# Four edits between the sub-layers of a two-layer trunk: tiles of their own for some weights, remainders on another engine, and the order of the norm's rows and squares

## The chip, the cores and the metric

The program runs on one core of a Trainium2 chip. The core has a matmul engine (PE, with weight loads shown apart as PEld), three engines for elementwise work (DVE or VectorE, ACT or ScalarE, POOL or GpSimd) and a queue that issues all transfers (SP). The metric is device time in microseconds (us) of one execution. The profile's times are counted from the first instruction of one profiled execution.

## The reference, cut to what matters

The trunk has two layers. Each has two sub-layers, a token mixer and an FFN, and around each stands a norm before and a norm behind:

```python
for l in range(DEPTH):
    h = _rmsnorm(x, pre_mix_norm[l])
    h = _hybrid_mixer(h, ...)
    x = x + _rmsnorm(h, post_mix_norm[l])
    h = _rmsnorm(x, pre_ffn_norm[l])
    h = _conv_glu_ffn(h, ffn_up[l], ffn_conv[l], ffn_conv_bias[l], ffn_down[l])
    x = x + _rmsnorm(h, post_ffn_norm[l])
```

`x` is 512 tokens by 1024 features in float32. The mixer's last step is a matmul with `w_out` (1024x1024), the FFN's first one is `ffn_up` (1024x5632) and its last one `ffn_down` (2816x1024). `_rmsnorm` divides each token's row by the root of its mean square, so nothing can be normed before the last feature of the matmul ahead of it is summed. That is the place the change is about: three transitions (mixer to FFN, FFN to the next layer's mixer, mixer to FFN) and the end of the program.

## The kernel before, in words

Features lie on the 128 partitions, tokens on the free axis. A weight unit is a tile of 128x1024 float32 numbers. It is loaded into one of two buffers `raw` (line 242), split by ACT into a rounded high half `whi` (line 146, 1 us) and by DVE or POOL into a remainder `wlo = raw - whi` (line 150). The pairs `whi`, `wlo` rotate through HL = 4 slots; a slot is free again once the matmuls have read the unit. An activation `hx` is split in the same way, and each product takes three matmuls (line 137): high by high, high by low, low by high.

**The transition.** A sub-layer's output has eight feature tiles `m` (`out_rows`). The last three of the mixer, and the last one of the FFN, are the *tail*: they are computed in two halves of 256 tokens, so that the norm of the first half can start while PE does the second. The steps of one half are: ACT squares the tail's sum into `vh` and DVE adds it to `acc`; PE sums `acc` over partitions (`pso<-cc,acc`); DVE and POOL make the inverse root (`rtp`); PE spreads it over the partitions (`pso<-cc,rtp`), and ACT copies it to the row `rs`. Then come eight rows `m` (function `row`): multiply by `rs` (tiles `A`, `B`, `C`, `psg`; DVE), add to `x` (tile `xt`; POOL for m = 1, 3, 5, else DVE), the high half of the next operand `hx` (ACT) and its low half (DVE, line 164). ACT also squares the new `x` for the norm that comes next (`sq`), and POOL adds the squares up (`acc<-acc,sq`).

The next sub-layer opens with its *lead*: three weight units into three PSUM tiles `pss`, half by half, while the operand tiles `hx` appear one by one. In the FFN of the profile these are 3 units x 8 tiles x 3 matmuls of 256 columns per half; in the mixer 16 small matmuls with `was` come to each half. The next norm's row (`rt`) is applied only when `pss` is read out. Behind the lead, PE goes on with units of 512 columns into four buffers `psg`.

**What sets the order.** The program is written out by a planner, `_Sched`: generators yield times, each operation has a cost, and the order in which they come out is the order on each engine. On the chip each engine works its list off in that order and waits for semaphores. So a change of costs or times in the planner moves instructions, and the chip's durations decide what these lists then wait for. In the planner a load lands 3.2 us after its issue. Around the transition the splitter sends a remainder to DVE or POOL, whichever is free sooner by the planner's count.

## Time and profile before

| | us |
|---|---|
| median of 3 runs | 1456.89 |
| the 3 runs | 1458.82, 1444.82, 1456.89 |
| the profiled execution | 1446.95 |
| its span, first to last instruction | 1445.2 |
| PE busy in it | 1388.6 |
| DVE busy | 949.3 |
| ACT busy | 610.1 |
| POOL busy | 593.2 |

The profiled execution is its span and 1.75 us around it. It is 9.94 us shorter than the median of the three runs, which lie 14 us apart. Busy times are sums over the whole span; the three transitions are about 30 us each, so a share of the span says little about them, and they are read from the timelines of the single engines.

### The profile page before, as it was taken

The numbers are of one execution on the slowest core, as the hardware profiler recorded it, in microseconds if no ns is written. First come the engines' busy times: TensorE is split into PE (matmuls) and PEld (weight loads), VectorE is DVE, ScalarE is ACT, GpSimd is POOL, SyncE is SP. The second block draws the span as 40 slices with busy tenths as digits, with TensorE's granted clock in tenths as the row PEclk, the third lists the DMA queues.
The fourth block names the chain that finished last, engine by engine and source line by source line (L and its number), as shares of the span: only waits on it lengthen the run. The fifth ranks groups of instructions, "written<-read, shape, count | busy, mean of one in ns | idle before, by whom it ended". The sixth has DMA issues, their size and how long they took to land.

```text
span 1445.2 us, 18826 instructions
## 1 busy us (share of the span) xinstructions
PE 1388.6 (96%) x7174; PEld 1147.8 (79%) x7174; DVE 949.3 (66%) x1503; ACT 610.1 (42%) x992; POOL 593.2 (41%) x359
## 2 busy tenths in 40 slices
PE   8999999998999999999999999999989999999996
PEld 5778766877888888888887877668878888888886
DVE  4785477667788788831379745668487888777213
ACT  4453356444544443332245434565355434443220
POOL 3344255314554444423343542543164544443332
PEclk9999999999999999999999999999999999999998
DMA  5233111032233223343332330110413333223331
GB/s 196 73 91 86 60 30 48 12 130 75 88 92 99 88 88 94 93 122 97 92 109 93 106 90 27 50 38 16 146 45 102 96 97 100 88 88 106 110 91 59
DMA packets 48698, 123.15 MB, mean 85 GB/s; under 512 B 15584, under 2 KB 18400, under 8 KB 48608
## 3 DMA queue, kind: packets, MB, share of 16 engines
q1 hardware_dynamic: 48608, 121.95, 27.7%
q8 instruction: 57, 0.93, 0.3%
q14 instruction: 33, 0.27, 0.1%
HBM read 115.11 MB, written 6.82 MB: 84 GB/s over the span
## 4 chain that ended last, share of the span: by engine, by line
PE 84%; DVE 12%; ACT 2%; issue 1%; DMA 0%; SPq 0%; POOL 0%; DVEq 0%; ACTq 0%
PE psg L137 70%; PE pss L137 9%; PE pso L137 2%; DVE kT L164 2%; DVE xt L150 1%; PE pss L142 1%; DVE A L150 1%; PE psg L142 1%; DVE hx L164 1%; DVE zt L150 1%; DVE qraw L164 1%; DVE C L150 1%; DVE rab L150 0%; DVE acc L150 0%; ACT whi L146 0%
## 5 line engine op out<-in xcount | busy, mean ns | idle before, releaser
L137 PE MATMUL psg<-hx,whi 128*128 128x512 f32 (+1 forms) x2080 | 629.0, 386 | 0.9 <-DVE C L157 0.8
L150 POOL TENSOR_TENSOR wlo<-raw,whi 128x1024 fp32r<-128x1024 f32 (+1 forms) x153 | 382.6, 2511 | 518.3 <-ACT whi L146 493.6
L137 PEld LDWEIGHTS psg<-hx,whi 128*128 128x128 f32 x2080 | 378.2, 189 | 78.2 <-issue 4.5
L137 PE MATMUL psg<-hx,wlo 128*128 128x512 f32 (+1 forms) x1040 | 396.2, 381 | 0.0
L146 ACT ACTIVATE whi<-raw 128x1024 fp32r<-128x1024 f32 (+1 forms) x208 | 215.5, 1036 | 262.9 <-PE psg L137 197.6
L164 DVE SCALAR_TENSOR_TENSOR B<-A,vv,B 128x510 f32<-128x510 f32 (+1 forms) x176 | 275.4, 1566 | 76.6 <-ACT B L146 73.5
L137 PEld LDWEIGHTS psg<-hx,wlo 128*128 128x128 f32 x1040 | 196.1, 189 | 38.0
L137 PE MATMUL psg<-hid,whi 128*128 128x512 f32 (+1 forms) x792 | 221.9, 366 | 0.0
L137 PEld LDWEIGHTS psg<-hid,whi 128*128 128x128 f32 x792 | 143.1, 189 | 24.3
L137 PE MATMUL psg<-hid,wlo 128*128 128x512 f32 (+1 forms) x396 | 144.8, 366 | 0.0
L150 DVE TENSOR_TENSOR wlo<-raw,whi 128x1024 fp32r<-128x1024 f32 (+1 forms) x55 | 70.6, 1286 | 109.0 <-ACT whi L146 108.9
L137 PE MATMUL psg<-whi,hx 128*128 128x512 f32 x384 | 123.7, 404 | 0.3 <-DVE A L150 0.3
L150 POOL TENSOR_TENSOR acc<-acc,sq 128x256 f32<-128x256 f32 (+1 forms) x65 | 68.1, 1048 | 103.8 <-ACT sq L146 100.7
L146 ACT ACTIVATE hid<-C 128x512 fp32r<-128x512 f32 x44 | 27.7, 630 | 179.5 <-DVE C L150 179.5
L137 PE MATMUL pss<-hx,whi 128*128 128x256 f32 (+1 forms) x336 | 82.3, 335 | 18.8 <-DVE hx L164 16.8
L137 PEld LDWEIGHTS psg<-hid,wlo 128*128 128x128 f32 x396 | 74.6, 189 | 12.2 <-POOL wlo L150 0.3
L137 PEld LDWEIGHTS pss<-hx,whi 128*128 128x128 f32 x336 | 61.9, 215 | 27.1 <-DVE hx L164 20.9
L146 ACT ACTIVATE B<-A,vv 128x512 f32<-128x512 f32 x88 | 71.0, 809 | 25.5 <-DVE A L150 24.5
L137 PEld LDWEIGHTS psg<-whi,hx 128*128 128x128 f32 x384 | 69.8, 190 | 13.6 <-DVE A L150 0.8
L137 PE MATMUL psg<-wlo,hx 128*128 128x512 f32 x192 | 75.7, 394 | 0.0
L150 DVE TENSOR_TENSOR A<-psg,rs 128x512 f32<-128x512 f32 x100 | 68.2, 683 | 2.0 <-POOL A L157 1.6
L137 PE MATMUL psg<-bT,bT 64*128 64x512 f32 (+3 forms) x128 | 48.2, 477 | 6.9 <-DVE nm L1170 4.2
(226 smaller groups left out, 1668.0 us busy)
## 6 DMA issues: line engine op xcount, KB each, us to landing
raw<-in_w_up_dram SPq DMA_DIRECT2D x88, 512.0 KB, 3.5
raw<-in_w_cm_dram SPq DMA_DIRECT2D x32, 512.0 KB, 3.6
raw<-in_w_dn_dram SPq DMA_DIRECT2D x32, 512.0 KB, 3.6
raw<-in_w_tm_dram SPq DMA_DIRECT2D x24, 512.0 KB, 3.5
raw<-in_w_o_dram SPq DMA_DIRECT2D x16, 512.0 KB, 3.5
raw<-in_w_dn_dram SPq DMA_DIRECT2D x16, 384.0 KB, 3.1
xt<-in_xT_dram SPq DMA_DIRECT2D x7, 512.0 KB, 6.7
scr_a<-am SPq DMA_DIRECT2D x8, 256.0 KB, 2.7
```

Source lines behind the costliest of these rows:

```text
L137: pe.matmul(ps, lhsT, rhs, start=start, stop=stop)
L142: pe.transpose(dst[:, i * P:(i + 1) * P], s, ident)
L146: nc.scalar.activation(out_, in_, func, **kw)
L150: (nc.vector if eng == "dve" else nc.gpsimd).tensor_tensor(out_, a, b, op=op)
L164: nc.vector.scalar_tensor_tensor(out_, a, s, b, op0=op0, op1=op1)
```

## The change

It has five parts. (1) Three weight units per layer, the lead of the FFN, get tiles of their own (`home`: the places of three mixer tiles that are done with once the scan is over), and the last unit of the FFN's down matmul gets a new tile `xu` of 2 x 768 columns; these four don't take a slot of the four. (2) From the end of the tail until the lead is done (`sc.chain`) every weight remainder goes to DVE. (3) The rows of a half start 1.1 us apart in the planner, not 0.6. (4) The squares for the next norm wait in the planner until all eight rows of their half are out. (5) The scratch of 16 KB per partition for another kind of transfer, of which the trace has none, is cut to 4 KB, to make room for `xu`.

```diff
@@ wseq
+        for i, tag in enumerate(("s7", "s5", "s1")):
+            home[len(wseq) + i] = (tag, (l, "scan", NC - 1))
         wseq += [(w_up[l, m], 1024) for m in range(2 * KF)]
...
+        home[len(wseq) - 1] = ("xu", None)
@@ splitter
-            yield from sc.get("wu", HL)
+            if u in home:
+                tag, flag = home[u]
+                if flag is not None:
+                    yield from sc.wait(flag)
+                if tag == "xu":
+                    pair = xp.tile([P, 2, 768], F32R, tag="xu", name="wxu")
+                else:
+                    pair = sp.tile([P, 2, 1024], F32R, tag=tag, name="whome")
+                hi, lo = pair[:, 0], pair[:, 1]
+            else:
+                yield from sc.get("wu", HL)
...
-            if len(wunit) > 1:
+            if sc.chain:
+                eng = "dve"
+            elif len(wunit) > 1:
                 eng = yield from sc.idle(("dve", "pool"), 1.5)
@@ square_sum
+        if key != "in":
+            yield from sc.wait(("rows", key, t0))
@@ lead
+        if last:
+            sc.chain = False
@@ out_rows, row
             left["m"] -= 1
+            left[t0] = left.get(t0, 8) - 1
+            if not left[t0]:
+                sc.set(("rows", key, t0))
@@ out_rows, chain
-                sc.spawn(row(m, seg, tail, r), 0, at=r + 0.6 * m)
+                sc.spawn(row(m, seg, tail, r), 0, at=r + 1.1 * m)
...
             sc.spawn(chain(seg, tail), 0)
+            sc.chain = True
@@ kernel
-    nc = _bacc.Bacc("TRN2", target_bir_lowering=False, num_devices=1)
+    nc = _bacc.Bacc("TRN2", target_bir_lowering=False, num_devices=1, dynamic_dma_scratch_size=4096)
```

How this moves instructions is seen at two transitions. The first is mixer to FFN in layer 0; the one in layer 1 differs from it in a few places only. On DVE, from the row `rs` of the first half to the first low half `hx`, there stood before:

```order
L150 TENSOR_TENSOR acc<-acc,vh 128x256
L150 TENSOR_TENSOR A<-A,rs 128x256
L150 TENSOR_TENSOR B<-B,rs 128x256
L157 TENSOR_SCALAR C<-psg,vv 128x256
L150 TENSOR_TENSOR C<-C,rs 128x256
L150 TENSOR_TENSOR xt_2717<-xt_2717,A 128x256
L150 TENSOR_TENSOR A<-A,rs 128x256
L150 TENSOR_TENSOR B<-B,rs 128x256
L150 TENSOR_TENSOR xt_2719<-xt_2719,C 128x256
L150 TENSOR_TENSOR acc<-acc,vh 128x256
L150 TENSOR_TENSOR C<-C,rs 128x256
L164 SCALAR_TENSOR_TENSOR hx_2842<-xt_2717,vv,hx_2842 128x256
```

And now:

```order
L151 TENSOR_TENSOR wlo<-raw,whi 128x1024
L151 TENSOR_TENSOR A<-A,rs 128x256
L151 TENSOR_TENSOR acc<-acc,vh 128x256
L151 TENSOR_TENSOR B<-B,rs 128x256
L151 TENSOR_TENSOR xt_2717<-xt_2717,A 128x256
L151 TENSOR_TENSOR wlo<-raw,whi 128x1024
L151 TENSOR_TENSOR C<-C,rs 128x256
L151 TENSOR_TENSOR acc<-acc,vh 128x256
L165 SCALAR_TENSOR_TENSOR hx_2842<-xt_2717,vv,hx_2842 128x256
```

Two remainders stand among the first rows (a third follows six instructions after the first `hx`), fewer rows are begun before the first `hx`, and the last addition to `acc` of the second half stands ahead of it.

On PE, the lead of the first half at the same transition (`pss_3065`, `3066`, `3067` are the three units' sums before; the rows go from the third quarter of the half on):

```order
L137 MATMUL pss_3065<-hx1_2843,whi_2854 128x256 x2
L137 MATMUL pss_3065<-hx1_2843,wlo_2855 128x256
L137 MATMUL pss_3066<-hx1_2843,whi_2966 128x256 x2
L137 MATMUL pss_3066<-hx1_2843,wlo_2967 128x256
...
L137 MATMUL pso_3109<-cc_80,rtp_3108 128x128 x2
L137 MATMUL pss_3067<-hx0_2842,whi_3006 128x256 x2
L137 MATMUL pss_3067<-hx0_2842,wlo_3007 128x256
```

The change's rows from the end of the tail on (`pss_3054`, `3055`, `3056` are the three units):

```order
L138 MATMUL pso_3074<-cc_80,acc_2622 128x1 x2
L138 MATMUL pss_3054<-hx0_2842,whome_2854 128x256 x3
L138 MATMUL pss_3055<-hx0_2842,whome_2880 128x256 x3
...
L138 MATMUL pss_3056<-hx0_2842,whome_2930 128x256 x6
L138 MATMUL pso_3074<-cc_80,rtp_3073 128x128 x2
L138 MATMUL pss_3054<-hx0_2842,whome_2854 128x256 x3
```

All three units are taken from the first operand tile on, and the second half's sum and its spread row stand ahead of the lead and behind 18 of its matmuls; before, they stood behind 24 and behind 54. (The first half's spread row went the other way: it stands 15 matmuls of the tail later.)

On POOL, at the same transition, before:

```order
L343 TENSOR_TENSOR rtp<-rtp,mhalf 128x2
L150 TENSOR_TENSOR xt_2717<-xt_2717,B 128x256
L150 TENSOR_TENSOR wlo<-raw,whi 128x1024
L150 TENSOR_TENSOR xt_2719<-xt_2719,A 128x256
L150 TENSOR_TENSOR xt_2721<-xt_2721,C 128x256
L150 TENSOR_TENSOR acc_2841<-acc_2841,sq 128x256 x2
```

And now:

```order
L361 TENSOR_TENSOR rtp<-rtp,mhalf 128x2
L151 TENSOR_TENSOR xt_2717<-xt_2717,B 128x256
L151 TENSOR_TENSOR xt_2719<-xt_2719,A 128x256
...
L151 TENSOR_TENSOR xt_2721<-xt_2721,C 128x256
...
L151 TENSOR_TENSOR acc_2841<-acc_2841,sq 128x256 x2
```

No remainder stands there any more, and the squares of the first half come behind that half's rows, among those of the second.

At the second transition (FFN of layer 0 to mixer of layer 1), PE behind the lead, before:

```order
L137 MATMUL psg<-hx_5633,whi 128x512 x2
L137 MATMUL psg<-hx_5633,wlo 128x512
L137 MATMUL pso<-cc,acc_5632 128x1 x2
...
L137 MATMUL pso<-cc,rt 128x128 x2
...
L687 MATMUL pso<-cc,C 128x16 x4
```

And now:

```order
L713 MATMUL pso<-cc,C 128x16 x4
...
L138 MATMUL pso<-cc,acc_5632 128x1 x2
L138 MATMUL psg<-hx_5634,whi 128x512 x2
L138 MATMUL psg<-hx_5634,wlo 128x512
...
L138 MATMUL pso<-cc,rt 128x128 x2
```

The spread of the next norm's row (`rt`) stands behind eight groups of three matmuls of 512 columns, where it stood behind four, and the four small matmuls on `C` now come ahead of it.

## Rows read from the trace of the kernel before

**Rows 1.** The page's part 1: busy us of each engine, its share of the span, and its instructions.

```profile
PE 1388.6 (96%) x7174; PEld 1147.8 (79%) x7174; DVE 949.3 (66%) x1503; ACT 610.1 (42%) x992; POOL 593.2 (41%) x359
```

**Rows 2.** The page's part 4, the chain of waits, by engine.

```profile
PE 84%; DVE 12%; ACT 2%; issue 1%; DMA 0%; SPq 0%; POOL 0%; DVEq 0%; ACTq 0%
```

**Rows 3.** Busy time by engine in three stretches, each from the end of one sub-layer's last matmul to the end of the next one's opening matmuls: mixer to FFN in layer 0, FFN of layer 0 to mixer of layer 1, mixer to FFN in layer 1. Columns: stretch, its length, busy us and instructions of PE, PE's weight loads, DVE, ACT and POOL, granted clock, DMA share, GB/s.

```profile
341.90:371.50 29.60, 23.09 (x161) 22.25 (x160) 23.50 (x43) 14.95 (x35) 20.11 (x23) 0.88 0.12 37
717.40:749.00 31.60, 26.81 (x193) 24.75 (x192) 26.22 (x43) 15.26 (x35) 19.48 (x22) 0.89 0.22 60
1055.60:1085.20 29.60, 23.01 (x161) 22.17 (x160) 23.52 (x43) 15.00 (x35) 20.18 (x23) 0.88 0.13 37
```

**Rows 4.** The timeline of PE in the first stretch; columns: start in us, duration in us (of all of a merged row), engine, line, operation, tiles, shapes, count, and in brackets the idle time before it and what ended that.

```profile
344.67 0.38 PE L137 MATMUL pss<-hx,whi 128*128 128x256 f32 x1 [2.64 <-DVE hx L164]
...
349.91 0.58 PE L137 MATMUL pso<-cc,acc 128*128 128x1 f32 x4 [0.66 <-DVE acc L150]
...
351.28 0.40 PE L137 MATMUL pss<-hx,whi 128*128 128x256 f32 x2
...
351.63 0.40 PE L137 MATMUL pss<-hx,whi 128*128 128x256 f32 x2
...
354.15 0.60 PE L137 MATMUL pso<-cc,rtp 128*128 128x128 f32 x4
...
360.49 0.39 PE L137 MATMUL pss<-hx,whi 128*128 128x256 f32 x1 [2.84 <-DVE hx L164]
...
371.54 0.63 PE L137 MATMUL psg<-hx,whi 128*128 128x512 f32 x2
```

**Rows 5.** Two pieces of the first stretch, columns as in rows 3.

```profile
344.00:349.00 5.00, 4.33 (x23) 4.29 (x23) 5.00 (x9) 3.31 (x8) 4.52 (x4) 0.66 0.18 72
349.00:357.00 8.00, 7.24 (x59) 6.78 (x57) 4.90 (x11) 2.73 (x8) 4.21 (x6) 1.00 0.21 68
```

**Rows 6.** The timeline of DVE in the first stretch.

```profile
336.09 1.23 DVE L150 TENSOR_TENSOR wlo<-raw,whi 128x1024 fp32r<-128x1024 f32 x1 [1.28 <-ACT whi L146]
...
337.57 0.42 DVE L150 TENSOR_TENSOR A<-A,rs 128x256 f32<-128x256 f32 x1
...
339.73 2.62 DVE L150 TENSOR_TENSOR A<-A,rs 128x256 f32<-128x256 f32 x1
...
344.14 0.47 DVE L164 SCALAR_TENSOR_TENSOR hx<-xt,vv,hx 128x256 fp32r<-128x256 f32 x1
...
347.49 2.27 DVE L150 TENSOR_TENSOR acc<-acc,vh 128x256 f32<-128x256 f32 x1
...
355.20 0.42 DVE L150 TENSOR_TENSOR A<-A,rs 128x256 f32<-128x256 f32 x1 [3.07 <-ACT rs L146]
...
365.93 1.37 DVE L164 SCALAR_TENSOR_TENSOR hx<-xt,vv,hx 128x256 fp32r<-128x256 f32 x3
```

**Rows 7.** The timeline of POOL in the first stretch, and the group of its additions of squares there (columns of the last: line, engine, operation, tiles, shapes, count, busy us, mean ns, idle before).

```profile
338.46 0.73 POOL L150 TENSOR_TENSOR xt<-xt,B 128x256 f32<-128x256 f32 x1 [2.84 <-PE psg L137]
...
339.43 2.63 POOL L150 TENSOR_TENSOR wlo<-raw,whi 128x1024 fp32r<-128x1024 f32 x1 [0.24 <-ACT whi L146]
...
344.30 0.91 POOL L150 TENSOR_TENSOR xt<-xt,C 128x256 f32<-128x256 f32 x1 [1.03 <-DVE C L150]
...
L150 POOL TENSOR_TENSOR acc<-acc,sq 128x256 f32<-128x256 f32 x13 | 11.0, 850 | 5.0 <-ACT sq L146 3.9 <-PE pss L137 0.7
```

**Rows 8.** Weight transfers: the page's part 6 (KB each, median us from issue to landing), and the spread of the landings from 300 to 345 us.

```profile
raw<-in_w_up_dram SPq DMA_DIRECT2D x88, 512.0 KB, 3.5
...
DMA to landing us min/median/max: 3.4/3.6/4.3
```

**Rows 9.** The timeline of PE in the second stretch and behind it.

```profile
719.92 0.39 PE L137 MATMUL pss<-hx,whi 128*128 128x256 f32 x1 [2.40 <-DVE hx L164]
...
749.00 0.63 PE L137 MATMUL psg<-hx,whi 128*128 128x512 f32 x2
...
752.28 0.71 PE L137 MATMUL pso<-cc,rt 128*128 128x128 f32 x4
...
778.48 2.05 PE L137 MATMUL pso<-cc,dn_g 128*128 128x128 f32 x8 [3.04 <-DVE edec L150]
```

**Rows 10.** The timeline of DVE and POOL in the second stretch.

```profile
716.39 2.62 DVE L150 TENSOR_TENSOR xt<-xt,C 128x256 f32<-128x256 f32 x1
...
738.90 2.62 DVE L164 SCALAR_TENSOR_TENSOR hx<-xt,vv,hx 128x256 fp32r<-128x256 f32 x4
...
753.44 1.29 DVE L150 TENSOR_TENSOR A<-pss,rs 128x512 f32<-128x512 f32 x2 [1.20 <-ACT rs L146]
...
716.36 2.37 POOL L150 TENSOR_TENSOR wlo<-raw,whi 128x1024 fp32r<-128x1024 f32 x1 [0.51 <-ACT whi L146]
```

**Rows 11.** The timeline of DVE in the third stretch.

```profile
1053.50 2.63 DVE L150 TENSOR_TENSOR A<-A,rs 128x256 f32<-128x256 f32 x1
...
1068.98 0.43 DVE L150 TENSOR_TENSOR A<-A,rs 128x256 f32<-128x256 f32 x1 [3.08 <-ACT rs L146]
```

**Rows 12.** The timeline of DVE at the end of the program.

```profile
1432.04 0.55 DVE L150 TENSOR_TENSOR acc<-acc,vh 128x256 f32<-128x256 f32 x1
...
1435.96 0.43 DVE L150 TENSOR_TENSOR A<-A,rs 128x256 f32<-128x256 f32 x1 [2.19 <-ACT rs L146]
...
1441.55 0.73 DVE L150 TENSOR_TENSOR xt<-xt,psg 128x256 f32<-128x256 f32 x2
```

More of the change, by code (lines that the diff above doesn't have):

```diff
@@ L56, in __init__ @@
         self.flags = {}
+        self.chain = False
     def spawn(self, gen, prio=1, at=0.0):
@@ L221 @@
     T_EXP, T_SILU, T_GELU = "exp_and_others", "silu_and_others", "gelu_apprx_tanh_and_others"
-    wseq = []
+    wseq, home = [], {}
     for l in range(DEPTH):
@@ L256, in splitter @@
             yield from sc.wait(("raw", u))
-            yield from sc.get("wu", HL)
+            if u in home:
[9 more added lines that the diff above has]
+                yield from sc.get("wu", HL)
+                hi = wp.tile([P, 1024], F32R, tag="hi", bufs=HL, name="whi")
+                lo = wp.tile([P, 1024], F32R, tag="lo", bufs=HL, name="wlo")
             raw = wraw.pop(u)
-            hi = wp.tile([P, 1024], F32R, tag="hi", bufs=HL, name="whi")
-            lo = wp.tile([P, 1024], F32R, tag="lo", bufs=HL, name="wlo")
             yield from sc.idle(("act",), 4.0)
@@ L277, in take, with free @@
         return wunit.pop(u)
-    def free(n=1):
+    def free(n=1, unit=None):
         for _ in range(n):
-            sc.put("wu", sc.t)
+            if unit not in home:
+                sc.put("wu", sc.t)
     def mm3(ps, wh, wl, xh, xl, first, last):
@@ L417, in lead @@
                     wunit.pop(units[i])
-                    free()
+                    free(unit=units[i])
             yield
+        if last:
+            sc.chain = False
     def out_rows(key, nt, rhs, nk, post, pre, dst, wait_rhs=None, flags=None):
@@ L505, in out_rows @@
             yield from done(m, ps)
-        us = []
+        us, u0 = [], wst["take"]
         for _ in range(nt * ((nk + 7) // 8)):
@@ L582, in out_rows @@
                     if seg[0] and (kt % 8 == 7 or kt == nk - 1):
-                        free()
+                        free(unit=u0 + i * nu + kt // 8)
                     yield
```

## The prediction

> **What bounds the kernel now.** I read the busy times first: PE works 1388.6 us, 96% of the span [rows 1], and the chain of waits gives it 84%, DVE 12%, ACT 2% [rows 2]. So the layers themselves are bound by PE, and the change leaves the number of large matmuls alone. It can win only where PE waits, and the three windows of the transitions show how much there is: 29.60, 31.60 and 29.60 us, with a granted clock of 0.88 to 0.89 [rows 3]. What would PE need there if nothing held it? A lead of the FFN is 48 groups of three matmuls (3 units, 8 tiles, 2 halves). Groups start 0.35 to 0.36 us apart where operands are ready [rows 4], so 48 x 0.36 = 17.3; the four short `pso` pieces (two sums, two spreads) add about 1.4 (0.58 and 0.60 are two of them [rows 4], the other two are shorter). That is 18.7 of 29.6: some 11 us are lost in the first stretch and as much in the third. The second stretch has 3.7 us more of PE's busy time (26.81 against 23.09 [rows 3]): 22.4 of 31.6, 9 lost.
>
> The timeline of PE says how they are lost: it starts at 344.67 behind an idle time of 2.64 that the first low half `hx` ended, and stops again for 2.84 at 360.49, for an `hx` of the second half [rows 4]. Behind the first gap the granted clock is 0.66, a mix of full speed (2.4 GHz) and half (1.2 GHz); from 349 on it is 1.00 [rows 5]. So DVE sets this end: its last low half `hx` is done at 365.93 + 1.37 = 367.30 [rows 6], and PE then has 4.24 us left to 371.54 [rows 4], twelve groups at 0.35.
>
> DVE loses time in three places there. A multiply of 128x256, 0.42 us at 337.57, takes 2.62 at 339.73, and an addition takes 2.27 at 347.49 [rows 6]. The first ends at 342.35, just behind GpSimd's remainder (339.43 + 2.63 = 342.06 [rows 7]). And DVE stands idle for 3.07 ahead of the second half's first row [rows 6]: the spread that it needs is issued by PE at 354.15 [rows 4], behind 54 matmuls of the lead, though PE's sum for it ran at 349.91 and its input `rtp<-pso` was done soon after.
>
> **The change part by part, first transition.** All sums run to the last `hx`, at 367.30 before.
> - Remainders off GpSimd: the long multiply and the long addition go back to about 0.4: 2.62 - 0.42 = 2.2 and 2.27 - 0.42 = 1.9, together -4.1.
> - The same remainders on DVE: three of them, 1.23 each [rows 6], 1.15 from start to start: +3.5. Taken as fully on the path, since DVE is the limiting engine.
> - Second half's spread behind 18 matmuls instead of 54: the idle 3.07 goes: -3.1. Its input hangs on the last `acc` addition, which now stands ahead of the first `hx`.
> - First half's spread stands 15 matmuls of the tail later, five groups by 0.36: +1.8 (one column count, the same duration).
> - Squares behind the rows: in the first half GpSimd's additions (mean 0.85, 13 in this stretch [rows 7]) no longer lie beside DVE's rows, some of which take 0.9 instead of 0.42. They now lie beside the second half's. Bounds 0 and -2; I take -0.8, nearer to nothing, since the work is moved and not removed.
> - Sum: -4.1 + 3.5 - 3.1 + 1.8 - 0.8 = -2.7, last `hx` at 364.6.
> - Behind it PE has less left. All three units are taken tile by tile now, so that only about two operand tiles are open: 2 x 3 x 0.36 = 2.2, not 4.24. The lead ends at 366.8 instead of 371.5: **4.7 us won**. PE alone, from an unchanged start near 344.7, would be done at 344.7 + 18.7 = 363.4, so DVE stays the limit.
>
> The third transition has the same rows (a multiply of 2.63, an idle time of 3.08 [rows 11]): 4.7 again.
>
> The pinned rows are also where the Trainium skill's page "SBUF — State Buffer", section "Who interferes with whom", can be held against the trace: a DVE instruction with two inputs in SBUF and a GpSimd instruction that reads SBUF share one read interface, and whichever came first holds off the other entirely. The long multiply agrees, ending 0.29 us behind GpSimd's remainder. The rule has a second side, which speaks against this change: a remainder on DVE has two such inputs too, and would hold off GpSimd; that is rival D.
>
> **Second transition.** The addition that took 2.62 at 716.39, beside a GpSimd remainder of 2.37 [rows 10], is freed: -2.2. That remainder on DVE costs 1.15 and perhaps 0.7 of waiting for its high half: +1.9. A remainder that stood among the second half's rows now stands behind the lead: -1.1. The squares: bounds 0 and -3, here -2.5, since before they lay beside the rows of both halves. Last `hx`: 738.90 + 2.62 = 741.5 before, 737.6 now. Now PE is the limit: from a start at 718.2 (719.92 [rows 9] less 1.7, the 2.2 with part of the remainder's cost back) 22.4 of work give 740.6, and I add 1.4 for the lower clock at the start [rows 5]: 742 against 749.00 [rows 9], 7.0 earlier. But the spread `rt`, which the readers of the lead need, stands behind four more groups. They took at most (752.28 - 749.00) / 4 = 0.82 each [rows 9]; I take 3.1 for the four. So DVE's first multiply behind the lead, at 753.44 [rows 10], comes only 3.9 earlier, and the chain from there to the stall of 3.04 at 778.48 [rows 9] moves with it; PE is there earlier and waits longer. **4.0 us won**, of 7.0.
>
> **The end.** The addition at 1432.04 comes some 0.85 earlier, but three more row operations stand behind the second row `rs` (1435.96, idle before it for 2.19 or less [rows 12]), at 0.37 each (0.73 for two [rows 12]) 1.1: between -0.8 and +1.1, taken as 0.
>
> **Costed at nothing.** Transfers: the loads are the same in number and size, landing 3.4 to 4.3 us after issue [rows 8]; SP's queue holds nothing new in front of them. Tiles of their own: ACT's high half no longer waits for a slot, and four free slots are filled while the lead runs; without that cover the first 512-column units would wait for a split, about 1 + 1.2 us. The later readout of the lead behind 3 units: covered by four buffers `psg`, each about 8 groups of 0.7 = 5.6 us of PE work; if that cover goes, about 1 us a transition. The squares' last addition stands shortly before PE's sum of them: a thin cover, also 1 us. The smaller scratch: the trace has no transfer that uses it; if it has any, nothing in the rows prices it.
>
> **Sum:** 4.7 + 4.0 + 4.7 = 13.4 us, from the profiled execution's 1446.95 to 1433.5. That execution is 9.94 shorter than the median of 1456.89. The four executions known lie at two levels, 1444.82 and 1446.95, 1456.89 and 1458.82, and I can't know on which the changed kernel's median falls; from their middle, 1451.9, I **predict 1439 us**, a gain of 0.9%. A measurement of this kernel can tell about 1% from no change, some 14.5 us.
>
> **Rivals.**
> - *B, more is won.* The squares account for all of their bound (2 a transition instead of 0.8), and `edec` at 778.48 does not hold the second transition back, so that its full 7.0 counts: 13.4 + 2.4 + 3.0 + about 1 for a clock that no longer drops = 20, time 1432. For it: of 29.6 us some 11 are lost, and I give back only 4.7. Against: the later `rt` is plainly in the order. Chance 0.15.
> - *D, DVE's remainders hold GpSimd's additions.* The rows m = 1, 3, 5 need an `xt` on GpSimd. If such an addition (0.73 and 0.91 now [rows 7]) starts only when a remainder on DVE has ended, up to 3 x 1.15 = 3.5 come back at each mixer-to-FFN transition, and 1.2 at the other: 13.4 - 8.2 = 5, time 1447. Against it: GpSimd's additions so far take no more than 0.91 beside a busy DVE, and the planner spaces the rows wider now. Chance 0.22. By the rule of the page named above this would be the expected case wherever the remainder starts first; the rows have only the other direction.
> - *C, slower: the weights come late.* The order puts DVE's remainders and ACT's high halves ahead of rows and of `hx`. Each waits for its transfer, and everything behind it on DVE waits too; on GpSimd such a wait held up little. Three loads in succession pass through the two `raw` buffers in such a stretch, so a landing that is x longer than 3.5 [rows 8] costs 3x at each of the two mixer-to-FFN transitions. It decides from 13.4 / 6 = 2.2, a landing of 5.7 us. At 7.0, twice the median, it costs 2 x 10.5 = 21: 8 slower than before, 1460; over 1% slower from a landing of 8.1. Against: the landings of this stretch are 3.4 to 4.3 with 37 GB/s in its window [rows 3, 8]. Chance 0.08.
>
> My forecast has the remaining 0.55.
>
> **Range and chances.** Low end: the lower level, 1445, less B's 20, 1425. High end: the upper level, 1458, less 4 (D with one mishap of 1 us), 1454. Outside stays C and the tails of the two levels. Faster by over 1%: B, and half of the forecast (its sum of 13.4 lies just below the bound): 0.15 + 0.27 = 0.42. Slower by over 1%: the worse half of C, 0.04. Within 1%: 0.54.
>
> **What would show it.** Right: no DVE row of 2.3 to 2.6 us in the three stretches, three remainders of 1.2 there, no idle time of 3 us ahead of the second half's first multiply, and stretches of about 25, 25 and 25 us. The second half's spread should follow its sum by under 3 us. In the second stretch `rt` should come some 6 us behind the lead's end, and the stall for `edec` grow by about 3. Wrong, by D: `xt` on GpSimd at 1.5 us and more, ending with a remainder. Wrong, by C: idle time on DVE ahead of a `wlo`, ended by ACT's `whi`, with landings above 5. Wrong in the base: stretches as short as said, but time lost elsewhere, above all at the first 512-column units or at PE's sum of the squares.

## The result, and the profile after

| | before | changed |
|---|---|---|
| median of 19 executions each | 1454.75 us | 1443.77 us |
| lowest and highest | 1444.17, 1464.74 | 1438.47, 1453.90 |
| ratio to before, 95% interval | | 0.9939 [0.9916, 0.9962] |
| profiled execution, its span | 1446.95, 1445.2 | 1443.73, 1441.7 |

The change makes the kernel faster by 0.61%, some 8.9 us of 1454.75 (5.5 to 12.2 by the interval). A second set of nine executions (e11 below) gave 0.9903 [0.9874, 0.9932]. The executions of the kernel before lie in two groups, near 1446 and near 1457; the last section shows what can make such a difference.

The two profiled executions are cut into pieces at marks on PE: the first 256-column matmul of a tail, and the first 512-column matmul behind a lead. "Stretch" is from the one to the other.

| piece, us | before | changed | difference | forecast |
|---|---|---|---|---|
| start to first tail (not changed) | 322.96 | 325.55 | +2.59 | 0 |
| stretch 1, mixer to FFN | 48.58 | 46.56 | -2.02 | -4.7 |
| FFN of layer 0 | 329.01 | 328.78 | -0.23 | 0 |
| stretch 2, FFN to mixer | 48.45 | 43.55 | -4.90 | -7.0 |
| mixer of layer 1 | 287.73 | 290.94 | +3.21 | +3.1 |
| stretch 3, mixer to FFN | 48.52 | 46.80 | -1.72 | -4.7 |
| FFN of layer 1 | 328.80 | 328.88 | +0.08 | 0 |
| last tail to last spread, and the rest | 31.15 | 30.64 | -0.51 | 0 |

Without the first piece that is 6.1 us. (The change doesn't touch that piece; a second profile of the changed kernel, e11, has 320.92 there, so its +2.59 is scatter.) The windows from the tail's end to the lead's end, columns as in [rows 3]:

```profile
345.20:372.10 26.90, 22.73 (x162) 21.16 (x161) 22.30 (x44) 13.97 (x35) 15.55 (x18) 0.94 0.16 51
717.70:744.40 26.70, 23.99 (x193) 22.20 (x192) 23.07 (x46) 15.09 (x35) 17.01 (x19) 1.00 0.16 41
1055.30:1082.20 26.90, 23.11 (x161) 22.17 (x161) 22.83 (x45) 13.11 (x32) 15.71 (x19) 0.87 0.19 60
```

They are 2.7, 4.9 and 2.7 shorter than in [rows 3]; the tails ahead of the first and the third are 0.7 and 1.0 longer. POOL has 4.6 us less to do in the first and DVE 1.2 less, although it took over the remainders: the rows that were pinned cost it more. The timeline of DVE in stretch 1, against [rows 6]:

```profile
339.49 1.23 DVE L151 TENSOR_TENSOR wlo<-raw,whi 128x1024 fp32r<-128x1024 f32 x1 [1.99 <-ACT whi L147]
340.63 0.15 DVE L160 TENSOR_SCALAR rtp<-pso 128x2 f32<-128x2 f32 x1
...
345.27 1.23 DVE L151 TENSOR_TENSOR wlo<-raw,whi 128x1024 fp32r<-128x1024 f32 x1 [0.82 <-ACT whi L147]
...
347.08 0.48 DVE L165 SCALAR_TENSOR_TENSOR hx<-xt,vv,hx 128x256 fp32r<-128x256 f32 x1
...
349.76 1.21 DVE L151 TENSOR_TENSOR wlo<-raw,whi 128x1024 fp32r<-128x1024 f32 x1
...
365.16 2.24 DVE L165 SCALAR_TENSOR_TENSOR hx<-xt,vv,hx 128x256 fp32r<-128x256 f32 x3
```

No row of 2.3 us is left, and no idle time of 3. But a remainder stands ahead of `rtp`, and DVE idles 1.99 in front of it, for ACT's high half. ACT in turn waited for the transfer:

```profile
338.39 1.06 ACT L147 ACTIVATE whi<-raw 128x1024 fp32r<-128x1024 f32 x1 [2.21 <-DMA raw<-in_w_up_dram]
```

PE had the sum for `rtp` ready at 337.65 + 0.58 = 338.2; DVE came to it at 340.63. What PE makes of it, against [rows 4]:

```profile
337.65 0.58 PE L138 MATMUL pso<-cc,acc 128*128 128x1 f32 x4
...
341.75 0.71 PE L138 MATMUL pso<-cc,rtp 128*128 128x128 f32 x4 [0.91 <-POOL rtp L361]
...
347.22 0.87 PE L138 MATMUL pso<-cc,acc 128*128 128x1 f32 x4 [1.89 <-DVE acc L151]
...
351.80 5.15 PE L138 MATMUL pss<-hx,whome 128*128 128x256 f32 x37
357.45 2.57 PE L138 MATMUL pss<-hx,whome 128*128 128x256 f32 x18 [0.50 <-DVE hx L165]
360.49 1.70 PE L138 MATMUL pss<-hx,whome 128*128 128x256 f32 x9 [0.47 <-DVE hx L165]
362.97 3.34 PE L138 MATMUL pss<-hx,whome 128*128 128x256 f32 x24 [0.78 <-DVE hx L165]
366.59 1.93 PE L138 MATMUL pss<-hx,whome 128*128 128x256 f32 x14 [0.28 <-DVE hx L165]
368.36 0.50 PE L138 MATMUL pso<-cc,acc 128*128 128x1 f32 x4
368.72 2.39 PE L138 MATMUL pss<-hx,whome 128*128 128x256 f32 x18
370.96 0.60 PE L138 MATMUL pso<-cc,rt 128*128 128x128 f32 x4
371.32 0.96 PE L138 MATMUL pss<-hx,whome 128*128 128x256 f32 x6
```

The lead is no longer stopped for 2.8 us, but PE still has some 32 matmuls and two short sums to do when the last `hx` is done at 365.16 + 2.24 = 367.40. And behind its wait for `acc` it runs at a lower clock again (0.59):

```profile
347.95:351.44 3.49, 3.49 (x19) 3.49 (x20) 3.49 (x7) 1.02 (x2) 3.41 (x3) 0.59 0.32 128
```

Behind the second lead, where 3.2 us are given back, PE, ACT and DVE show this:

```profile
763.93 1.01 PE L138 MATMUL pso<-dn_g,cc 128*128 128x16 f32 x4 [4.20 <-DVE dn_g L165]
```

```profile
751.58 0.38 ACT L147 ACTIVATE rs<-pso 128x256 f32<-128x256 f32 x1 [5.08 <-PE pso L138]
754.89 1.06 ACT L147 ACTIVATE whi<-raw 128x1024 fp32r<-128x1024 f32 x1 [2.93 <-DMA raw<-in_w_cm_dram]
755.85 0.19 ACT L147 ACTIVATE dn_ea<-rc 128x4 f32<-128x4 f32 x1
```

```profile
751.99 1.29 DVE L151 TENSOR_TENSOR A<-pss,rs 128x512 f32<-128x512 f32 x2 [1.43 <-ACT rs L147]
756.18 2.29 DVE L158 TENSOR_SCALAR dn_beta<-dn_beta 128x16 f32<-128x16 f32 x1 [2.90 <-ACT dn_beta L147]
```

DVE's first multiply behind the lead comes 7.55 us behind the lead's end, not 4.44 as before (753.44 - 749.00 [rows 9, 10]). Two things follow it that the order of before didn't have: ACT's split of a late unit in front of the gate's small operations, and a `dn_beta` of 2.29 us instead of 0.17. The stall of 3.04 at 778.48 [rows 9] is gone; one of 4.20 stands earlier. Which of these counts is a question for the runs.

### The profile page after: what moved, and what is told of

Its sections match the earlier page's. It is cut to its first block, busy times and chain, and to the rows that moved or that the text cites. A ratio compares the mean times of both kernels' runs of the same rounds, so it can differ in the third digit from the quotient of the medians.

```text
span 1441.7 us, 18796 instructions
## 1 busy us (share of the span) xinstructions
PE 1386.2 (96%) x7174; PEld 1143.9 (79%) x7174; DVE 940.9 (65%) x1512; ACT 613.0 (43%) x992; POOL 566.6 (39%) x350
## 5 line engine op out<-in xcount | busy, mean ns | idle before, releaser
L151 POOL TENSOR_TENSOR wlo<-raw,whi 128x1024 fp32r<-128x1024 f32 (+1 forms) x142 | 355.6, 2515 | 510.3 <-ACT whi L147 490.5
L147 ACT ACTIVATE whi<-raw 128x1024 fp32r<-128x1024 f32 (+1 forms) x200 | 207.7, 1038 | 261.4 <-PE psg L138 196.5
L165 DVE SCALAR_TENSOR_TENSOR B<-A,vv,B 128x510 f32<-128x510 f32 (+1 forms) x176 | 265.6, 1511 | 70.2 <-ACT B L147 66.9
L138 PE MATMUL psg<-hid,whi 128*128 128x512 f32 (+1 forms) x744 | 213.4, 371 | 0.0
L138 PEld LDWEIGHTS psg<-hid,whi 128*128 128x128 f32 x744 | 135.7, 188 | 24.2
L151 DVE TENSOR_TENSOR wlo<-raw,whi 128x1024 fp32r<-128x1024 f32 (+1 forms) x58 | 75.7, 1307 | 111.7 <-ACT whi L147 111.5
L138 PE MATMUL psg<-hid,wlo 128*128 128x512 f32 (+1 forms) x372 | 137.9, 371 | 0.0
L138 PEld LDWEIGHTS psg<-hid,wlo 128*128 128x128 f32 x372 | 70.1, 188 | 11.9
L147 ACT ACTIVATE C<-B 128x512 f32<-128x512 f32 x44 | 27.8, 632 | 71.3 <-DVE B L165 71.3
L158 POOL TENSOR_SCALAR B<-B,den 128x512 f32<-128x512 f32 (+1 forms) x30 | 41.2, 1375 | 30.2 <-DVE den L177 17.4
```

The source lines that it names most:

```text
L138: pe.matmul(ps, lhsT, rhs, start=start, stop=stop)
L147: nc.scalar.activation(out_, in_, func, **kw)
L151: (nc.vector if eng == "dve" else nc.gpsimd).tensor_tensor(out_, a, b, op=op)
L158: e.tensor_scalar(out_, a, s1, None, op0=op0)
L165: nc.vector.scalar_tensor_tensor(out_, a, s, b, op0=op0, op1=op1)
```

## The experiments

Two theories. **DVE's first half**: in the mixer-to-FFN transitions units that nobody needs yet are split among the rows, and delay `rtp`, `hx` and the lead. **PE itself**: its clock and its own amount of work set the end. For the second transition: the row `rs`, or the late split on ACT. The pieces of all profiles (stretches 1, 2, 3, the mixer of layer 1, and all from the first tail to the last spread):

| run | 1 | 2 | 3 | mixer 1 | all | ratio to before |
|---|---|---|---|---|---|---|
| before | 48.6 | 48.5 | 48.5 | 287.7 | 1111.3 | |
| changed | 46.6 | 43.6 | 46.8 | 290.9 | 1105.1 | 0.9939 |
| e1 | 52.0 | 44.4 | 50.9 | 291.1 | 1115.8 | 0.9985 [0.9953, 1.0018] |
| e2 | 43.9 | 45.1 | 42.0 | 291.0 | 1100.3 | 0.9853 [0.9811, 0.9895] |
| e3 | 46.5 | 43.6 | 46.6 | 291.1 | 1105.1 | 0.9940 [0.9908, 0.9973] |
| e4 | 46.6 | 46.4 | 46.7 | 298.6 | 1115.6 | 0.9899 [0.9838, 0.9961] |
| e5 | 44.2 | 44.4 | 44.2 | 290.4 | 1103.5 | one execution, 1439.27 us |
| e6 | 47.9 | 45.7 | 48.7 | 300.6 | 1120.8 | one execution, 1457.96 us |
| e7 | 50.1 | 44.9 | 48.8 | 300.3 | 1121.2 | one execution, 1457.55 us |
| e8 | 44.1 | 45.1 | 41.7 | 298.2 | 1107.2 | 0.9920 [0.9884, 0.9956] |
| e9 | 46.1 | 44.3 | 46.1 | 294.0 | 1108.2 | one execution, 1441.99 us |
| e10 | 44.0 | 45.0 | 41.8 | 290.9 | 1100.0 | 0.9874 [0.9837, 0.9910] |
| e11 | 47.0 | 43.6 | 46.6 | 291.0 | 1105.5 | 0.9903 [0.9874, 0.9932] |
| e12 | 42.5 | 46.4 | 42.1 | 298.4 | 1107.7 | 0.9904 [0.9871, 0.9938] |

Where a column says nearly 300, the execution had the long spell at half clock of the last section; that piece is not a measure of the edit then.

**e1, remainders to either engine again.**

```diff
-            if sc.chain:
-                eng = "dve"
-            elif len(wunit) > 1:
+            if len(wunit) > 1:
```

> The changed kernel with its part (2) undone: between the end of the tail and the end of the lead the planner again picks DVE or GpSimd for each remainder. Measured in the profile from the first 256-column matmul of the tail to the first 512-column matmul behind the lead, the kernel before has 48.6, 48.5 and 48.5 us in the three transitions, the changed one 46.6, 43.6 and 46.8. Theory 1 (GpSimd's remainders pin DVE rows for 2.3 to 2.6 us each, and that is worth the move): two pinned rows come back in each mixer-to-FFN transition, about 2 x 2.0 minus the two remainders of 1.15 that DVE is rid of, so 47.5 to 49 us there, time 1 to 5 us above the changed kernel. Theory 2 (the move to DVE gave nothing, since the remainders now stand ahead of the rows on DVE, one of them ahead of the first half's rtp): 45 to 46.5 us, time 0 to 3 us below the changed kernel.

Measured: stretches of 52.0 and 50.9, more than theory 1 allowed, and so is the time, 1451.61 by the median, 7.8 above the changed kernel where 1 to 5 were expected. Undone alone, part (2) costs 5.5 and 4.1: with the other parts in place the mixer-to-FFN transitions are then worse than before the change. DVE and POOL:

```profile
334.64 2.41 DVE L151 TENSOR_TENSOR acc<-acc,vh 128x256 f32<-128x256 f32 x1 [0.79 <-ACT vh L147]
...
347.35 2.38 DVE L165 SCALAR_TENSOR_TENSOR hx<-xt,vv,hx 128x256 fp32r<-128x256 f32 x1
```

```profile
334.41 2.35 POOL L151 TENSOR_TENSOR whome<-raw,whome 128x1024 fp32r<-128x1024 f32 x1 [13.84 <-ACT whome L147]
...
346.99 2.45 POOL L151 TENSOR_TENSOR wlo<-raw,whi 128x1024 fp32r<-128x1024 f32 x1 [3.40 <-ACT whi L147]
```

Each long DVE row lies over a remainder on POOL (the second ends at 349.73, the remainder at 349.44). One of them is now an `hx` that PE waits for.

**e9, part (2) alone, on the kernel before.**

```diff
+            if sc.chain:
+                eng = "dve"
-            if len(wunit) > 1:
+            elif len(wunit) > 1:
...
+        if last:
+            sc.chain = False
...
             sc.spawn(chain(seg, tail), 0)
+            sc.chain = True
```

> The kernel before with part (2) alone: from the end of the tail to the end of the lead every remainder goes to DVE; no tiles of its own for any unit, rows 0.6 apart, squares among the rows. One look, read by the stretch from the tail's start to the lead's end in the mixer-to-FFN transitions (before 48.6 and 48.5). Theory 1 (my sum: two pinned rows go, 4.1, three remainders come, 3.5): 47 to 48.5, almost nothing, since the idle 3.1 ahead of the second half stays (its spread still stands behind most of the lead). Theory 2 (the remainders' move is the larger part of the change, as undoing it made the stretches 52.0 and 50.9): 44.5 to 46.5.

Measured: 46.1 and 46.1, theory 2. Part (2) alone gives the mixer-to-FFN transitions all that the whole change gives them (46.6 and 46.8), by one execution. What it does not give is the second transition: 44.3 there, but 294.0 behind it, 2.1 longer than before over both.

**e5, e6, e7, the other parts undone one at a time.** In e5 `home` stays empty, in e6 the rows start 0.6 apart, in e7 the squares don't wait:

```diff
-            home[len(wseq) + i] = (tag, (l, "scan", NC - 1))
+            pass
...
-        home[len(wseq) - 1] = ("xu", None)
```

```diff
-                sc.spawn(row(m, seg, tail, r), 0, at=r + 1.1 * m)
+                sc.spawn(row(m, seg, tail, r), 0, at=r + 0.6 * m)
```

```diff
-        if key != "in":
-            yield from sc.wait(("rows", key, t0))
```

> The changed kernel with its part (1) undone: no unit has a tile of its own, all rotate through the four slots; the rest of the change stays. One look; the reading is the stretch from the tail's start to the lead's end in the two mixer-to-FFN transitions (before 48.6 and 48.5, changed 46.6 and 46.8). Theory 1 (tiles of their own let all three units of the lead be split before the tail is over, and that is what lets the order keep the second half's spread early): the lead waits for its third unit again, 48 to 50 us. Theory 2 (the own tiles only let the splitter run ahead, and with it put the remainders into the first half's rows; without them the first half is freer): 44.5 to 46.5 us.

> The changed kernel with its part (3) undone: rows of a half start 0.6 us apart in the planner, as before. One look, read by the stretches (changed: 46.6, 43.6, 46.8). Theory 1 (in sequence, the first hx comes earlier by the rows that are no longer begun ahead of it, about two rows of 0.34): the lead starts about 0.7 later and the stretches grow by 0.5 to 1.5 us each. Theory 2 (the spacing only changes order within a DVE list that is full either way): within 0.4 us of the changed kernel in all three.

> The changed kernel with its part (4) undone everywhere: the squares for the next norm come among the rows again. One look, read by the stretches (changed: 46.6, 43.6, 46.8; with the squares among the rows behind the FFN alone: 46.4 in the second). Theory 1 (GpSimd's additions beside DVE's rows cost about 0.8 on the first half's path and little else): stretches 1 and 3 grow by 0.5 to 1.5 us, the second is 46.4 again. Theory 2 (they cost the full bound, 2 and more): 48.5 us and more in stretches 1 and 3.

Measured: without the spacing 1.3, 2.1 and 1.9 more (theory 1 or a little over it), without the late squares 3.5, 1.4 and 2.0 more: 50.1 and 48.8 in the mixer-to-FFN transitions, as theory 2 has it. (The second transition took 44.9 there, not the 46.4 that theory 1 took over from e4, where the same part is undone behind the FFN only; why is open.) Without tiles of their own the stretches are *shorter*, 44.2 and 44.2 (theory 2, even below its range): with only the four slots no remainder stands right ahead of `rtp` (the last ends 6 us before it). Three still come behind it, two of them ahead of the first `hx`, but that `hx` is done 18.7 us behind the tail's start, not 22.0. It is paid back behind the lead in part: the FFN of layer 0 takes 331.1 instead of 328.8, that of layer 1 329.6 instead of 328.9. Over both pieces e5 is equal in layer 0 and 1.9 better in layer 1. So in the changed kernel's order parts (3) and (4) help and part (1) costs stretch; beside e9's 46.1 the three together give the mixer-to-FFN transitions nothing on top of part (2).

**e2 and e10, later units held back.** A unit behind the three of the lead is split only when the second half's rows are out:

```diff
             yield from sc.wait(("raw", u))
+            while sc.hold is not None and u >= sc.hold:
+                yield sc.t + 0.2
...
+                if key[1] == "m" and t0:
+                    sc.hold = None
...
             sc.chain = True
+            if key[1] == "m" and not seg[0]:
+                sc.hold = wst["take"] + 3
```

> The changed kernel, and from the end of the first half of the mixer's tail the splitter holds back every unit behind the three of the lead until the second half's rows are out. No remainder then stands among the rows, and none ahead of rtp, which in the changed kernel waited behind a remainder from 338.2 to 340.63. Theory 1 (what kept the mixer-to-FFN transitions from gaining 4.7 is DVE's first half: a remainder ahead of rtp costs 2.2, three among the rows 1.15 each; PE's start of the lead is late by as much, and after it PE has the backlog): the lead starts 2.5 to 4 us earlier behind the tail's start, and the stretch falls from 46.6 and 46.8 to 42 to 44 us in both; time 5 to 9 us below the changed kernel. Theory 2 (PE itself, at a lower clock behind its gap, or the second half's chain, sets the end): the stretch stays within 1.5 us of 46.7. Theory 3 (the units held back are missed behind the lead): PE waits 2 us and more for a remainder at the first 512-column units.

Measured: 43.9 and 42.0, and 7.9 and 4.8 us under the changed kernel by the medians of two sets (1435.83 and 1435.57 against 1443.77 and 1440.40; the second pair ran on one chip). Theory 1. `rtp` is no longer behind a remainder, and the lead follows the tail without a gap:

```profile
334.85 0.16 DVE L161 TENSOR_SCALAR rtp<-pso 128x2 f32<-128x2 f32 x1 [0.76 <-PE pso L139]
```

```profile
340.59 3.46 PE L139 MATMUL pss<-hx,whome 128*128 128x256 f32 x24
...
352.86 0.39 PE L139 MATMUL pss<-hx,whome 128*128 128x256 f32 x1 [1.09 <-ACT hx L148]
354.39 7.53 PE L139 MATMUL pss<-hx,whome 128*128 128x256 f32 x35 [1.14 <-DVE hx L166]
```

The tail began at 321.98, so the lead starts 18.6 behind it, not 22.4. Theory 3 holds in a small part: PE waits once in the FFN for a remainder, for 0.7, and that piece is 1.0 longer. What is now left of stretch 1 is theory 2's: PE gets ahead of DVE, waits at 352.86 and 354.39, and then does its work at half clock:

```profile
352.00:356.00 4.00, 2.00 (x7) 1.54 (x7) 4.00 (x6) 2.28 (x6) 3.29 (x4) 0.75 0.00 0
356.00:360.00 4.00, 3.91 (x19) 3.87 (x19) 3.24 (x9) 2.40 (x8) 1.78 (x2) 0.50 0.00 0
```

The second transition, where this edit holds nothing, takes 45.1, 1.5 more than in the changed kernel: its granted clock is 0.93 from 718 to 742, where the changed kernel had 1.00 throughout, and its row `rs` comes 52.3 behind the tail's start, as late as before the change.

> The run that held back the units behind the lead, once more, beside the changed kernel on the same chip. By the profiles' stretches it should be 3 to 5 us below the changed kernel (43.9 and 42.0 against 46.6 and 46.8, less 1.0 behind the first lead and 1.5 of a lower clock in the second transition). Theory 1: ratio to before 0.985 to 0.990. Theory 2 (the first reading, 0.9853 from four executions, was luck in where the long stretch at half clock in layer 1's mixer fell): 0.990 to 0.994.

Measured: 0.9874 [0.9837, 0.9910] and stretches of 44.0 and 41.8: theory 1, the first reading was no luck. This kernel beats both, the one before by 1.3 to 1.5%.

**e3, one unit held behind the second lead** (and with it those that the splitter takes after it).

```diff
         us = reserve(3)
+        if l:
+            sc.hold = us[0] + 6
...
             r = act(t1, t1, AF.Exp, after=r)
             yield r
+            sc.spawn(unhold(r + 1.6), 0)
```

> The changed kernel, with one weight unit of the second transition (the sixth behind its lead's first) held back in the splitter until the small gate operations on ACT have been issued; squares and spread stay as in the changed kernel. From the lead's end in the second transition to the tail of layer 1 the kernel before takes 287.7 us, the changed one 290.9: 3.2 of the 4.9 won in that transition are given back. Theory 1 (ACT's split of that unit waits 2.93 us for its transfer, ahead of dn_beta and dn_t, and the GpSimd remainders that then follow pin dn_beta and dn_t on DVE for 2.3 and 2.2 us): PE's stall of 4.20 ahead of pso<-dn_g at 763.93 shrinks below 2, no 2 us rows on dn_beta and dn_t, and 290.9 falls to 287.5 to 289; time 2 to 3.5 us below the changed kernel. Theory 2 (my prediction: it is the late spread rt that gives it back): the piece stays at 290 to 291.5, as the spread has not moved.

Measured: theory 1's signs came (the stall at `pso<-dn_g` shrank to 1.21, `dn_beta` took 0.17), and the time did not: 291.1, as theory 2 has it. The wait that was taken away came back 17 us later:

```profile
758.12 0.59 PE L139 MATMUL pso<-dn_g,cc 128*128 128x16 f32 x4 [1.21 <-DVE dn_g L166]
775.12 1.83 PE L139 MATMUL pso<-cc,dn_g 128*128 128x128 f32 x8 [3.80 <-DVE edec L152]
```

**e4, squares among the rows behind the FFN only.**

```diff
-        if key != "in":
+        if key != "in" and key[1] == "m":
```

> The changed kernel with its part (4) undone behind the FFN only: in the second transition the squares come among the rows, as before, and the spread rt stands earlier (seven of PE's rows behind the sum, the four small matmuls on C behind it). The mixer-to-FFN transitions are as in the changed kernel. Theory 1 (late rt and what ACT does around it cost 3.2 behind the lead; the squares among the rows cost DVE 2 to 3 in it): the stretch of the second transition grows from 43.6 to 44.5 to 46.5, the piece behind it falls from 290.9 to 287.5 to 288.5, and the time is about the same, 2 us to either side. Theory 2 (the late squares are what shortened the second transition): 46 to 48 us there, and nothing is won behind it that is not lost in front, time up to 2 us above the changed kernel.

Measured: the stretch is 46.4, within both theories. The piece behind it is spoilt by the long spell at half clock, but up to the last `pso<-cc,dn_g` it can be read: 40.4 us behind the lead's end, as before the change (40.5), against 43.6 in the changed kernel. So what is lost in front is won behind, as theory 1 has it. Both ends together: 86.8 behind the tail's start, 87.1 in the changed kernel, 88.9 before. Taken from the row `rs`, that mark comes 36.4 us later in the kernel before, 36.4 in the changed one, 36.7 in e3, 36.5 in e4, 36.5 in e2, while the lead's end moves by 4.9. So the second transition is worth what `rs` gains, which is 1.8 (52.48 to 50.69 behind the tail's start), and not what the lead gains.

**e8, `rs` earlier.** e2 and e3 together, and in the second mixer the gate waits for the row `rs`, and so for the spread `rt`, before its four matmuls on `C`, which share one PSUM buffer with the sum:

```diff
         def gates():
+            if l:
+                yield from sc.wait(*ready)
             ps = yield from pget("o")
```

> Three edits on the changed kernel: units behind the lead held back until the mixer's rows are out (as in the run that held them), the sixth unit of the second transition held until the gate operations are issued, and in that transition the four small matmuls on C put behind the spread rt, so that the sum of the squares no longer waits for the one PSUM buffer they share. Theory 1 (behind the second lead everything hangs on the row rs: in the kernel before, the changed one and the runs on it the last pso<-cc,dn_g comes 36.4 to 36.7 us after rs, while the lead's end lies anywhere from 43.6 to 48.5 behind the tail's start): rs comes at 48.5 to 49.2 behind the tail's start instead of 50.1 to 50.7, and the last pso<-cc,dn_g at 85 to 86 instead of 86.8 to 87.1. Theory 2 (the chain of the gates, not rs, sets it; with C's matmuls later it starts later): 87 to 90. Mixer-to-FFN stretches 42 to 44 as in the run that held the units. Time about 1434, ratio to before 0.983 to 0.988.

Measured: theory 2. `rs` came at 50.3, and the mark at 88.1, now 37.8 behind `rs`: with `C`'s matmuls behind the spread the gate's own chain starts later, and takes the place of `rs`. So `rs` sets that piece only as long as the gate's chain is ready with it. The time missed its forecast too: 1442.46 and 0.9920, not 1434 and 0.983 to 0.988; the profile has the long spell.

**e11 and e12.** The changed kernel once more, and e2's edit with e4's.

> The changed kernel once more, for a second profile of it. Theory 1 (the transitions repeat to 0.1 us, and what scatters between executions is how long PE runs at half clock in the mixer of layer 1): stretches 46.6, 43.6 and 46.8 within 0.15 us, and the piece from the second lead to the tail of layer 1 either near 291 or near 300. Theory 2 (the transitions scatter by a microsecond too): they differ by 0.5 us and more from the first profile.

> Two edits on the changed kernel: the units behind the lead held back until the mixer's rows are out (1435.8 and 1435.6 in two runs), and the squares of the second transition among the rows, as before the change. Theory 1 (both parts add: stretches 43.9 and 42.0 in the mixer-to-FFN transitions, and in the second one the last pso<-cc,dn_g at 86.8 behind the tail's start instead of 88.7, where that held kernel lost 1.5 to a lower clock in its lead): 1.5 to 2 us below the held kernel, ratio to before 0.983 to 0.988. Theory 2 (the clock takes it back, the lead of the second transition being longer with squares among the rows): no better than the held kernel, 0.986 to 0.991.

Measured: e11 has 47.0, 43.6 and 46.6, so stretches 2 and 3 repeat to 0.03 and 0.2, and stretch 1 to 0.43 only: between the two theories. In e12 the parts do add in the stretches (42.5 and 42.1, the mark at 86.8), but the ratio, 0.9904, is not better than e2's, which is theory 2's figure; the profile puts it down to the clock, though in the mixer and not in the lead.

## Why the prediction was right or wrong

The time, 1443.8, lies in the range of 1425 to 1454, the direction is right, and "within 1%" had the largest chance. The sum was too large: 13.4, where the pieces show 6.1 and the ratio 8.9. That the time still came within 5 us of 1439 is in part luck: the 2.8 by which the ratio exceeds the pieces are no term of the sum, and the last section has only a guess at them.

- **Remainders off GpSimd, -4.1: right.** The pinned rows are gone, and e1 brings such rows back.
- **The same remainders on DVE, three of them, +3.5: right, and one missed.** Behind `rtp` three stand: the first is over when `rs` comes, the second costs 1.15 and an idle time of 0.82 in front of it, the third 1.15: 3.1. A fourth stands ahead of `rtp`, a place that I had not looked at on DVE's list.
- **The first half's spread, +1.8: too small, 3.2.** It comes 16.20 behind the tail's start instead of 13.02. I counted PE's five groups and not the remainder on DVE that waits for ACT, which waits for its transfer; PE waits 0.91 for it. That is rival C's mechanism with little of its cause: the transfer took 4.2 (others in this stretch 3.4 to 3.7), and it was issued only at 334.17, when DVE's remainder of an own tile (332.92, 1.23 long) had given a `raw` buffer back. It costs 1.4, not the 10.5 of that rival.
- **The idle 3.07: gone, as forecast,** though the second half's spread follows its sum by 4.2 (347.22 to 351.44), not by under 3.
- **The last `hx`: right in sum, by errors that cancel.** -2.7 forecast; 44.34 behind the tail's start before, 41.85 now: -2.5. The four terms above come to -0.9 as measured, not -1.9; the rest of -1.6 is left to the squares and to what the sum didn't hold.
- **"DVE sets this end", and "behind it PE has less left", 2.2 instead of 4.24: wrong, and this is the step that failed.** From the last `hx` to the lead's end it took 4.71 (367.40 to 372.11). The sum ran to a point for which PE didn't wait, in the kernel before either. There PE's last wait ends at 360.49 [rows 4], and from then on it is busy without a gap, for 11.05 us, at a granted clock of 0.85 (columns as in [rows 3]):

```profile
360.49:371.54 11.05, 11.05 (x80) 11.04 (x81) 8.02 (x16) 6.89 (x15) 7.62 (x9) 0.85 0.00 1
```

  In the changed kernel the last wait ends at 366.59, and 5.52 us of work at full clock follow:

```profile
366.59:372.11 5.52, 5.52 (x46) 5.52 (x47) 0.98 (x2) 1.88 (x6) 4.29 (x6) 1.00 0.00 0
```

  Counted from the tail's start, that wait ends 3.5 later (41.04, not 37.53), and the work behind it is 5.5 shorter: the 2.0 of the table. I let PE start "unchanged near 344.7", 21.7 behind the tail's start, run at full clock and wait for nothing but the last tiles. It started 22.4 behind, ran 3.5 us at 0.59, stood still for four gaps of 2.0 in all, and so had a backlog. Its need of 18.7 was a bound, not its time: 24.2. e2, with the start at 18.6, shows what was to be had, 4.7 and 6.5 of stretch.
- **Second transition: the mechanism right, one size off.** PE began 1.6 earlier (forecast 1.7), at full clock throughout, but it waited for `hx` in pieces: the lead's end came 4.9 earlier, not 7.0. The give-back, 3.1 forecast, was 3.2, so 1.7 were won, not 4.0. e3 and e4 bear out the reason: not the late split on ACT that looks so plain in the trace, but the row `rs`. Rival B's premise, that the full 7.0 counts, fell with it.
- **Rival D: its mechanism is there, its size is not.** Against it I had said that GpSimd's additions took no more than 0.91 beside a busy DVE. The trace of the kernel before has four of 1.18 to 1.42 that start during a remainder on DVE; one of them, with that remainder:

```profile
369.52 1.42 POOL L150 TENSOR_TENSOR acc<-acc,sq 128x256 f32<-128x256 f32 x1 [0.74 <-PE pss L137]
369.11 1.23 DVE L150 TENSOR_TENSOR wlo<-raw,whi 128x1024 fp32r<-128x1024 f32 x1 [1.82 <-ACT whi L146]
```

  In the changed kernel two additions on an `xt` take longer in stretch 1:

```profile
348.03 1.53 POOL L151 TENSOR_TENSOR xt<-xt,A 128x256 f32<-128x256 f32 x1 [2.97 <-issue]
...
350.38 1.19 POOL L151 TENSOR_TENSOR xt<-xt,C 128x256 f32<-128x256 f32 x1
```

  Only the second meets a remainder (349.76 to 350.98); the first is over before it and lies beside DVE's short rows. That is some 1.1 us in all, not 3.5, on rows that no longer end the stretch.
- **Squares, -0.8 between 0 and -2: too small.** Undone, they cost 3.5 and 2.0 of stretch (e7), if only in the changed kernel's order, where other rows stand beside them.
- **The end, 0:** -0.5.
- **Tiles of their own, costed at nothing: wrong.** They are what lets a remainder in ahead of `rtp`; e5 has them cost 2.3 and 2.6 of stretch, and give back 2.4 and 0.8 behind the lead.

The rows show who waits for whom between DVE and GpSimd in both directions. In the fourteen profiles 63 of GpSimd's additions (128x256) start during a remainder on DVE, and each ends 0.58 to 0.61 us behind that remainder, whenever it started; of 68 DVE rows of 128x256 that start during a remainder on GpSimd, 63 end 0.28 or 0.29 behind it, among them e1's of 2.41 and 2.38, and the other five take one input from `psg`, in PSUM. (Counted are those with over 0.1 us of the remainder to come.) By the Trainium skill, "SBUF — State Buffer", section "Who interferes with whom", a DVE instruction with two SBUF inputs and a GpSimd instruction that reads SBUF exclude each other, the one that issues second waiting until the first is done. The trace agrees, by these numbers.

## What to carry to other kernels

When a wait is taken off an engine's list, read the whole list from the first thing the critical chain needs on it, also ahead of the place that is edited: here one early instruction in front of a 0.15 us operation cost 1.4 us, where each freed row gave about 2. More buffers let a producer run ahead, and what it does early then stands in front of what is urgent; hold it back by what is needed next, not by what is free. Before a sum is run to an engine's last result, check that the next engine still waits for it there: PE's last wait was 7 us earlier. A stage's gain is worth only what reaches the next thing waited for: measure from mark to mark, past the stage.

## What the runs showed of the hardware

**Half clock for long in one place.** The profiles whose mixer of layer 1 takes nearly 300 us lose it in one place. Two kernels with much the same instructions there, e12 and e10, some 119 us behind the second lead's end:

```profile
861.00:885.00 24.00, 24.00 (x126) 19.77 (x126) 5.66 (x20) 6.05 (x11) 0.64 (x1) 0.50 0.01 5
```

```profile
862.00:886.00 24.00, 24.00 (x180) 18.43 (x179) 11.00 (x36) 8.09 (x18) 3.81 (x2) 0.89 0.14 43
```

PE is busy all the time in both; at a granted clock of 0.50, the level of 1.2 GHz, it gets 126 matmuls done, at 0.89 it gets 180. Half clock sets in near this place, 115 to 122 us behind the lead's end, in thirteen of the fourteen profiles; it lasts 20.5 to 27.3 us in e4, e6, e7, e8 and e12 and at most 6.8 in the others. With the long spell the piece is 298.2 to 300.6, in the other runs on the changed kernel 290.4 to 291.1. (Two of the long executions were timed by themselves, at 1457.96 and 1457.55.) The kernel before has two groups that differ in the same way: beside the runs it was timed 69 times, 17 times at 1444.2 to 1450.3 us with a mean granted clock of 0.976 to 0.980, otherwise at 1453.8 and more with 0.972 and less. From 0.977 to 0.969 is, as an estimate, 0.008 x 1455 / 0.5 = 23 us more at half clock, the length of such a spell; where it lies isn't shown, as no execution of the longer group was profiled.

What goes with the spell is the stall behind the second lead: in the seven profiles where PE waits 3.95 us or more at `pso<-dn_g` (the changed kernel, e1, e2, e5, e9, e10, e11) it is short; in the seven where it doesn't and waits later, for `edec`, it is long in five. That would explain why e8 and e12, with shorter transitions, are no faster than e2, and why the changed kernel's median gains more than its 6.1. It is a coincidence of fourteen profiles, not an experiment. e3 comes nearest to one, as it moves that stall and leaves the stretches as they were: six of its ten executions took over 1447 us, at 0.971 to 0.977, against five of the changed kernel's 28. But its one profile has no long spell, so where the others lost their time isn't shown.

**A pinned operation with one input.** `dn_beta<-dn_beta`, 128x16, took 2.29 us beside a GpSimd remainder, 0.17 without; it ended at 758.47, the remainder at 758.44. By the Trainium skill, "SBUF — State Buffer", section "Who interferes with whom", an operation with one tensor input can be held off as well, where it runs in a mode that uses the shared ports. The row fits that; in which mode it ran, no run shows.
